# Adaptive-norm modulation in steps of 512 columns and a state-space recurrence whose backward half runs in reversed time, on one Trainium2 core

## The chip, the core and the metric

The kernel runs on one core of a Trainium2 chip. The core has a matrix engine (TensorE, PE in the rows), a vector engine (VectorE, DVE), an activation engine (ScalarE, ACT), GpSimd (POOL) and SyncE (SP), which here only issues loads. Each engine works through its own instructions in order and meets the others at semaphores. The metric is the device time of one execution in microseconds (us); smaller is better.

## What is computed

Two layers of a diffusion backbone, for 128 context tokens and 256 latent tokens (384 columns together), 1024 channels wide. Cut to what the change touches:

```python
def ada_mods(cvec, p):
    m = jax.nn.silu(cvec) @ p['ada_w'] + p['ada_b']          # 1024 x 6144 weights
    return jnp.split(m[:, None, :], 6, axis=-1)

def trunk_layer(x, cvec, p, mixer_fn):
    sh1, sc1, g1, sh2, sc2, g2 = ada_mods(cvec, p)
    mixed, extra = mixer_fn(rmsnorm(x, p['norm1_g']) * (1 + sc1) + sh1)
    x = x + g1 * mixed
    x = x + g2 * conv_ffn(rmsnorm(x, p['norm2_g']) * (1 + sc2) + sh2, p)
    return x, extra

# inside the mixer, beside three kinds of attention: a complex diagonal recurrence in both directions
for d, rev in enumerate((False, True)):
    a_re, a_im, bb_re, bb_im = s5_discretize(...)
    y_d, f_re, f_im = s5_direction(u, a_re, a_im, bb_re, bb_im, c_re, c_im, h0[:, d, 0], h0[:, d, 1], rev)
    y = y + y_d
```

The modulation is a product of two vectors (context and latent) with 1024 x 6144 weights in each layer. The recurrence has 16 groups of 64 complex states in each direction.

## The kernel before

One program handles both token sets at once: activations lie channel by channel, 128 channels on the partitions and 384 tokens along the free axis. A layer is a mixer (input projection, four head groups, output projection) and a gated MLP. Large products are done three times (`mm3`, L296 to L299): weights and activations are split into a high and a low part, and three matmuls of 384 or 386 columns add up. `split1` makes the two parts of a weight piece, the high one on ACT (L289), the low one on DVE (L290).

**Modulation.** The weights of a third of a layer's modulation (group g, 1024 x 2048) are loaded by SP in 16 pieces of 128 x 1024 (512 KB), into three buffers of the tag `ada`. `ada_steps` (L315 to L333) is a generator: one step loads a piece and issues four fp32 matmuls of 256 columns on it, whose 32-column stationary operands stand in the four column quarters of the array, so that four weights columns are worked on at once (L320). There are five such groups (80 steps); the sixth, the first third of layer 0, is done at the start in `first` by `mod` (L1413) on tiles of the tag `a0`, of which there are `NA0`.

**Recurrence.** Time is cut into steps of eight tokens, `NC` = 51 columns with pads. The forward direction lies on partitions 0 to 63, the backward one on 64 to 127. For each of four blocks of four groups, `states` (L774) multiplies the block's input with a table (eight fp32 matmuls of 51 columns with a 128 x 128 stationary operand, L779), rotates the result (L789 to L791), puts in the initial states, and runs four `tensor_tensor_scan` on DVE: real and imaginary part, forward (L797) and backward from the end (L799), on 64 partitions each. `outputs` (L814) turns states into tokens. The rotation and decay tables are made once in each layer by `s5_rot` (L644), which copies three of them with ACT (L659 to L661); layer 0's are made in the prologue, layer 1's during the MLP of layer 0.

**Order.** In the prologue (`first`) PE, ACT, DVE and SP follow the order of the code. In the mixer a string (`SPEC[l]`) sets which generator takes its next step: A is a modulation step, G a projection, N, Q and M the attention groups, S the recurrence, T its tables. Within that a scheduler places instructions by priorities; `adjacent` keeps a list of matmuls next to each other. Loads on SP and on GpSimd's queue start in order, each when its buffer is free.

Of the kernel before, what the change touches and what calls it, by code (L numbers as in the profile page):

```python
# [12 lines left out]
F32 = mybir.dt.float32  # L13
F32R = mybir.dt.float32r
I32 = mybir.dt.int32
AF = mybir.ActivationFunctionType
OP = mybir.AluOpType
# [3 lines left out]
L = 2  # L21
# [8 lines left out]
NC = 51  # L30
# [27 lines left out]
NA0 = 5  # L58
# [3 lines left out]
NADA = 3  # L62
# [7 lines left out]
SPEC = ['AATGTATAGGGTTTTGTATAGGGNGAGAANAGGNASNANNNASNAGAAASNGSATNSAANMGGNAGASQANSSQMQSAAAQMAMQAQMQMSAMAAAQASNQAAQQMQMAMAAAQSSSAQMMMMMAAAQMMAMAAAAM', 'SGAGAGSGASGAASNSGGSSGSNAGSAGAGNSSMNNANNGSNNGANSGQGNQASAMGAAQQGQNQQMNMQAQNMMQMAAAMAAQQQMAMQMAQAAAMMAM']  # L70
# [59 lines left out]
def _prepare(a):  # L130
    f = np.float32
    a = {n: np.asarray(v) for n, v in a.items()}
# [5 lines left out]
    def col(v, p=128):  # L138
        return v.reshape(-1, p).T

    r = {}
# [4 lines left out]
    r["ada"] = np.stack([w.reshape(8, 128, 4, 2, 256).transpose(0, 3, 1, 2, 4)  # L146
                         for l in range(L) for w in np.split(a["ada_w"][l], 3, axis=1)][1:]
                        ).reshape(5, 8, 2, 128, 1024)
# [69 lines left out]
def _program(tc, I, O):  # L218
# [95 lines left out]
    def ada_steps(l, g):  # L314
        acc = pa()  # L315
        for kc in range(8):
            for h in range(2):
                raw = piece(I["ada"][3 * l + g - 1, kc, h], 1024, "ada")
                for c in range(4):
                    PE.matmul(acc[32 * c:32 * c + 32, 256 * h:256 * h + 256], cw[:, kc],  # L320
                              raw[:, 256 * c:256 * c + 256], start=kc == 0 and h == 0,
                              stop=kc == 7 and h == 1)
                if kc < 7 or h == 0:
                    yield
        ar = kp.tile([128, 512], F32, name="ar", tag="sqz", bufs=3)
# [318 lines left out]
    def s5_rot(l, w, w4, qp, cmp):  # L644
# [14 lines left out]
        A.activation(w4[0], w[0], AF.Copy)  # L659
        A.activation(w4[1], w[1], AF.Copy)  # L660
        A.activation(w4[2], w[1], AF.Copy, scale=-1.0)  # L661
# [4 lines left out]
        V.memset(rt[64:128, :, 17:51:33], 0.0)  # L666
# [75 lines left out]
    def s5_steps(l, st, sp_):  # L742
# [28 lines left out]
        def states(b):  # L771
# [4 lines left out]
            for i in range(2):  # L776
                for g in range(4):
                    q = 4 * i + g
                    PE.matmul(e[:, NC * q:NC * q + NC], E[:, 128 * q:128 * q + 128], U[:, 4 * b + g], start=True,  # L779
                              stop=True)  # L780
# [12 lines left out]
            V.tensor_copy(t1[64:128, :, :, 50], HR[l][64:128, :, gs])  # L793
            gt = tmp("g")
            r3 = W[:, 3].rearrange("p g m -> p (g m)")
            for i in range(2):
                V.tensor_tensor_scan(gt[0:64, i].rearrange("p g m -> p (g m)"), r3[0:64],  # L797
# [777 lines left out]
```

## Time and profile before

| | |
|---|---|
| median of 3 runs | 1107.12 us (1101.26 to 1111.03) |
| the profiled execution's own time | 1107.33 us |
| its span | 1105.5 us |
| PE busy | 1065.4 us, 96% of the span |
| DVE busy | 795.7 us, 72% |
| ACT busy | 580.7 us, 53% |
| POOL busy | 88.3 us, 8% |

The span is the time from the first to the last instruction of one execution. Busy time of an engine counts each moment once, also where several of its instructions overlap. An fp32 matmul stands in the trace as two records, one of the split products and a transpose as one.

### The profile page before, as it was taken

How to read it: one execution, taken by the hardware profiler on the slowest of the kernel's cores; microseconds unless marked ns; L12 is line 12 of the kernel's file. 1: busy time of each engine (PE TensorE's matmuls, PEld its weight loads, DVE VectorE, ACT ScalarE, POOL GpSimd, SP SyncE). 2: the span in 40 equal slices, each digit the busy share in tenths (PEclk: the TensorE clock that was granted, in tenths of full speed). 3: DMA queues.
4: the chain of work that ended last, by engine and by line, in shares of the span. 5: the costliest groups of instructions: out<-in, count | busy, mean ns of one | idle time of the engine just before them, and what ended most of it. 6: DMA issues, size and time to landing. Idle time of an engine off the chain costs nothing.

```text
span 1105.5 us, 18673 instructions
## 1 busy us (share of the span) xinstructions
PE 1065.4 (96%) x6724; PEld 909.4 (82%) x6724; DVE 795.7 (72%) x1998; ACT 580.7 (53%) x1251; POOL 88.3 (8%) x201
## 2 busy tenths in 40 slices
PE   6798999999999999999999989899999999999998
PEld 3587475457999999999999877545799999999998
DVE  6897476778899864678966877557769775476753
ACT  3753445545676543455556645574568553355532
POOL 4212221000100000001110210100000000000000
PEclk8999898999999999999999999999999999999999
DMA  9987776555545334445455774436333434534343
GB/s 337 304 283 282 200 227 219 168 186 201 166 146 179 120 100 142 135 132 150 144 137 158 215 249 136 106 130 215 101 117 97 134 116 118 148 120 129 111 134 99
DMA packets 64700, 182.19 MB, mean 165 GB/s; under 512 B 15840, under 2 KB 19168, under 8 KB 64608
## 3 DMA queue, kind: packets, MB, share of 16 engines
q1 hardware_dynamic: 55456, 152.52, 44.1%
q0 software_dynamic: 8576, 28.16, 8.4%
q8 instruction: 53, 0.87, 0.3%
q10 hardware_dynamic: 576, 0.32, 0.1%
q14 instruction: 39, 0.32, 0.1%
HBM read 166.19 MB, written 14.78 MB: 164 GB/s over the span
## 4 chain that ended last, share of the span: by engine, by line
PE 81%; DMA 6%; DVE 6%; issue 4%; ACT 2%; POOL 1%; SPq 0%; DVEq 0%; POOLq 0%; ACTq 0%
PE pz L297 12%; PE pz L299 12%; PE pz L298 12%; PE psc L299 9%; PE psc L298 8%; PE psc L297 8%; PE pa L320 4%; PE psc L955 3%; DMA raw<-ada 2%; PE ptr L959 1%; PE po L974 1%; DMA tbw<-sw 1%; PE psc L779 1%; DVE lo L290 1%; DMA sf<-ca 1%
## 5 line engine op out<-in xcount | busy, mean ns | idle before, releaser
L289 ACT ACTIVATE hi<-raw 128x512 fp32r<-128x512 f32 (+2 forms) x396 | 228.1, 585 | 275.4 <-PE pz L298 111.9
L290 DVE TENSOR_TENSOR lo<-raw,hi 128x512 fp32r<-128x512 f32 (+2 forms) x396 | 250.8, 636 | 147.9 <-ACT hi L289 105.0
L299 PE MATMUL pz<-ah,lo 128*128 128x386 f32 (+1 forms) x616 | 211.6, 344 | 3.3 <-DVE lo L290 3.2
L297 PE MATMUL pz<-ah,hi 128*128 128x386 f32 (+1 forms) x616 | 214.7, 350 | 0.1
L298 PE MATMUL pz<-al,hi 128*128 128x386 f32 (+1 forms) x616 | 212.7, 346 | 0.0
L297 PEld LDWEIGHTS pz<-ah,hi 128*128 128x128 f32 x616 | 117.5, 191 | 15.7 <-issue 12.7
L299 PEld LDWEIGHTS pz<-ah,lo 128*128 128x128 f32 x616 | 117.6, 191 | 8.8 <-issue 4.5
L298 PEld LDWEIGHTS pz<-al,hi 128*128 128x128 f32 x616 | 117.9, 191 | 3.6 <-issue 2.1
L299 PE MATMUL psc<-ah,lo 128*128 128x386 f32 (+1 forms) x336 | 114.7, 341 | 0.1
L298 PE MATMUL psc<-al,hi 128*128 128x386 f32 (+1 forms) x336 | 114.8, 342 | 0.0
L297 PE MATMUL psc<-ah,hi 128*128 128x386 f32 (+1 forms) x336 | 114.7, 341 | 0.0
L299 PEld LDWEIGHTS psc<-ah,lo 128*128 128x128 f32 x336 | 63.9, 190 | 1.0 <-DVE lo L290 0.4
L297 PEld LDWEIGHTS psc<-ah,hi 128*128 128x128 f32 x336 | 64.2, 191 | 0.3 <-ACT hi L289 0.3
L298 PEld LDWEIGHTS psc<-al,hi 128*128 128x128 f32 x336 | 64.2, 191 | 0.2 <-issue 0.2
L320 PE MATMUL pa<-raw,cw 128*32 128x256 f32 x640 | 60.1, 394 | 4.2 <-DMA raw<-ada 3.9
L297 PE MATMUL pz<-fh,hi 128*128 128x384 f32 x176 | 59.5, 338 | 0.1
L299 PE MATMUL pz<-fh,lo 128*128 128x384 f32 x176 | 59.4, 338 | 0.0
L297 PE MATMUL psc<-fh,hi 128*128 128x384 f32 x176 | 59.4, 338 | 0.0
L299 PE MATMUL psc<-fh,lo 128*128 128x384 f32 x176 | 59.3, 337 | 0.0
L298 PE MATMUL pz<-fl,hi 128*128 128x384 f32 x176 | 59.2, 336 | 0.0
L298 PE MATMUL psc<-fl,hi 128*128 128x384 f32 x176 | 59.1, 336 | 0.0
L932 ACT ACTIVATE P<-P,ty 128x384 f32<-128x384 f32 (+1 forms) x72 | 38.9, 540 | 37.1 <-DVE P L931 25.5
(425 smaller groups left out, 1937.0 us busy)
## 6 DMA issues: line engine op xcount, KB each, us to landing
raw<-wup SPq DMA_DIRECT2D x88, 512.0 KB, 3.6
raw<-ada SPq DMA_DIRECT2D x80, 512.0 KB, 4.5
raw<-win SPq DMA_DIRECT2D x30, 512.0 KB, 5.0
raw<-wdn SPq DMA_DIRECT2D x32, 384.0 KB, 3.1
raw<-wdn SPq DMA_DIRECT2D x32, 320.0 KB, 2.9
a<-ada SPq DMA_DIRECT2D x16, 512.0 KB, 6.2
raw<-wout SPq DMA_DIRECT2D x16, 512.0 KB, 3.6
se<-tbo POOLq DMA_DIRECT2D x16, 256.0 KB, 3.6
```

What stands on the lines that cost most here:

```text
L289: A.activation(hi[:, :n], raw[:, a:b], AF.Copy)
L290: V.tensor_tensor(lo[:, :n], raw[:, a:b], hi[:, :n].bitcast(F32), op=OP.subtract)
L297: PE.matmul(out, wh, xh, start=start, stop=False)
L298: PE.matmul(out, wh, xl, start=False, stop=False)
L299: PE.matmul(out, wl, xh, start=False, stop=stop)
L320: PE.matmul(acc[32 * c:32 * c + 32, 256 * h:256 * h + 256], cw[:, kc], raw[:, 256 * c:256 * c + 256], start=kc == 0 and h == 0, stop=kc == ...
L779: PE.matmul(e[:, NC * q:NC * q + NC], E[:, 128 * q:128 * q + 128], U[:, 4 * b + g], start=True, stop=True)
L932: A.activation(P[:, :w], P[:, :w], AF.Exp, bias=mn, scale=-1.0, accum_out=rs)
L955: PE.matmul(S[:, :T], qf(1 + qb), kf(128, 512), start=True, stop=True)
L959: PE.transpose(tr[:, 128 * kb:128 * kb + 128], P[:, 128 * kb:128 * kb + 128], ident)
L974: calls.append(lambda kb=kb, j=j: PE.matmul(o[64 * j:64 * j + 64, 128:T], heads[j][2](1 + kb), PTs[j][1][:, kb].rearrange("p q c -> p (q c ...
```

## The change

Modulation: `ada_steps` now waits for the two pieces of a row of weights and then issues four matmuls of 512 columns, kept adjacent, every second step; the host packs the weights to suit. Prologue: of the 16 tiles of the first modulation third every third one goes to the buffers of the tag `ada`, the others to four (five before) of the tag `a0`. Recurrence: the backward half is held in reversed time. The table matmul is split into two of 64 stationary columns, the second reading the input backwards; one scan over all 128 partitions takes the place of a forward and a backward one; the rotation tables are copied in halves, the upper one reversed; the result is turned back where it is read. Both strings of `SPEC` are new.

```diff
@@ -55,7 +55,7 @@
 LAG = 2
 LATE = 7
 CM2 = 0
-NA0 = 5
+NA0 = 4
 NAH = 9
 NPT = 3
 NRAW = 3
@@ -67,7 +67,7 @@
 LNP = ()
 LOWP = 300
 LOWA = 3000
-SPEC = ['AATGTATAGGGTTTTGTATAGGGNGAGAANAGGNASNANNNASNAGAAASNGSATNSAANMGGNAGASQANSSQMQSAAAQMAMQAQMQMSAMAAAQASNQAAQQMQMAMAAAQSSSAQMMMMMAAAQMMAMAAAAM', 'SGAGAGSGASGAASNSGGSSGSNAGSAGAGNSSMNNANNGSNNGANSGQGNQASAMGAAQQGQNQQMNMQAQNMMQMAAAMAAQQQMAMQMAQAAAMMAM']
+SPEC = ['TTAGTGTAATTGTAATAGAGGTNAAAGGANAANGGNNAGAGAGSGANNSSAAANMNGSASQNNNNNTSGAAAQAGASSMQQSAMMQQMQASAMQAQMMSAQMAQASQAQAAAQMSMAASAAMMAMMMAMQMAMAAAA', 'SSSAAGAGAAGGSSGGASNSGASNAGGSGGSSMNNSANNGNNGQNANSGQNASAMGAAQQQQMNMQGMNQAGAMMAAQAAAQNQQMQMAQMMAQMAAAMM']
 
 WIN_COLS = [
     np.arange(768, 896), np.arange(896, 1024),
@@ -143,9 +143,8 @@
     r["xT"] = pk(x.T)
     cc = np.stack([a["c_ctx"], a["c"][0]], 1)
     r["cT"] = pk(cc)
-    r["ada"] = np.stack([w.reshape(8, 128, 4, 2, 256).transpose(0, 3, 1, 2, 4)
-                         for l in range(L) for w in np.split(a["ada_w"][l], 3, axis=1)][1:]
-                        ).reshape(5, 8, 2, 128, 1024)
+    r["ada"] = np.stack([w.reshape(8, 128, 2, 1024).transpose(0, 2, 1, 3)
+                         for l in range(L) for w in np.split(a["ada_w"][l], 3, axis=1)][1:])
     r["ada0"] = a["ada_w"][0][:, :2048].reshape(2, 4, 128, 2, 8, 128).transpose(4, 0, 2, 1, 3, 5).reshape(8, 2, 128, 1024)
     r["win"] = np.stack([np.stack([pk(a["w_in"][l][:, c]) for c in WIN_COLS]
                                   + [pk(a["w_in"][l][h * 512:(h + 1) * 512, 512:768]) for h in range(2)])
@@ -314,14 +313,16 @@
     def ada_steps(l, g):
         acc = pa()
         for kc in range(8):
+            raw = []
             for h in range(2):
-                raw = piece(I["ada"][3 * l + g - 1, kc, h], 1024, "ada")
-                for c in range(4):
-                    PE.matmul(acc[32 * c:32 * c + 32, 256 * h:256 * h + 256], cw[:, kc],
-                              raw[:, 256 * c:256 * c + 256], start=kc == 0 and h == 0,
-                              stop=kc == 7 and h == 1)
-                if kc < 7 or h == 0:
+                raw.append(piece(I["ada"][3 * l + g - 1, kc, h], 1024, "ada"))
+                if h == 0:
                     yield
+            adjacent([lambda c=c: PE.matmul(acc[32 * c:32 * c + 32], cw[:, kc],
+                                            raw[c // 2][:, 512 * (c % 2):512 * (c % 2) + 512], start=kc == 0,
+                                            stop=kc == 7) for c in range(4)])
+            if kc < 7:
+                yield
         ar = kp.tile([128, 512], F32, name="ar", tag="sqz", bufs=3)
         V.tensor_copy(ar, acc)
         tr = pt()
@@ -656,14 +657,14 @@
             yield from cmul_steps([v[:, :, h + 1:h + 1 + n] for v in w], [v[:, :, 1:1 + n] for v in w],
                                   [v[:, :, h:h + 1].to_broadcast(shp) for v in w], shp, cmp)
             h += n
-        A.activation(w4[0], w[0], AF.Copy)
-        A.activation(w4[1], w[1], AF.Copy)
-        A.activation(w4[2], w[1], AF.Copy, scale=-1.0)
+        for v, u, c in ((w4[0], w[0], 1.0), (w4[1], w[1], 1.0), (w4[2], w[1], -1.0)):
+            A.activation(v[0:64], u[0:64], AF.Copy, scale=c)
+            A.activation(v[64:128], u[64:128, :, ::-1], AF.Copy, scale=c)
         rt = w4[3]
         V.tensor_copy(rt, rho[:, lg, None].to_broadcast([128, 16, NC]))
         yield
         V.memset(rt[0:64, :, 0:18:17], 0.0)
-        V.memset(rt[64:128, :, 17:51:33], 0.0)
+        V.memset(rt[64:128, :, 0:34:33], 0.0)
         yield
         for i in range(4):
             G.dma_start(SW[l][:, :, 4 * NC * i:4 * NC * i + 4 * NC], w4[i].rearrange("p (b g) m -> p b (g m)", b=4))
@@ -776,8 +777,9 @@
             for i in range(2):
                 for g in range(4):
                     q = 4 * i + g
-                    PE.matmul(e[:, NC * q:NC * q + NC], E[:, 128 * q:128 * q + 128], U[:, 4 * b + g], start=True,
-                              stop=True)
+                    for d in range(2):
+                        PE.matmul(e[64 * d:64 * d + 64, NC * q:NC * q + NC], E[:, 128 * q + 64 * d:128 * q + 64 * d + 64],
+                                  U[:, 4 * b + g, ::1 - 2 * d], start=True, stop=True)
             e4 = e[:, :w8].rearrange("p (i g m) -> p i g m", i=2, g=4)
             wc = W[:, 0:1].to_broadcast([128, 2, 4, NC])
             ws = W[:, 1:3]
@@ -790,21 +792,18 @@
             V.tensor_tensor(t2, e4[:, ::-1], ws, op=OP.mult)
             V.tensor_tensor(t1, t1, t2, op=OP.add)
             V.tensor_copy(t1[0:64, :, :, 17], HR[l][0:64, :, gs])
-            V.tensor_copy(t1[64:128, :, :, 50], HR[l][64:128, :, gs])
+            V.tensor_copy(t1[64:128, :, :, 0], HR[l][64:128, :, gs])
             gt = tmp("g")
             r3 = W[:, 3].rearrange("p g m -> p (g m)")
             for i in range(2):
-                V.tensor_tensor_scan(gt[0:64, i].rearrange("p g m -> p (g m)"), r3[0:64],
-                                     t1[0:64, i].rearrange("p g m -> p (g m)"), 0.0, op0=OP.mult, op1=OP.add)
-                V.tensor_tensor_scan(gt[64:128, i].rearrange("p g m -> p (g m)")[:, ::-1], r3[64:128, ::-1],
-                                     t1[64:128, i].rearrange("p g m -> p (g m)")[:, ::-1], 0.0, op0=OP.mult,
-                                     op1=OP.add)
+                V.tensor_tensor_scan(gt[:, i].rearrange("p g m -> p (g m)"), r3,
+                                     t1[:, i].rearrange("p g m -> p (g m)"), 0.0, op0=OP.mult, op1=OP.add)
             t1, t2 = tmp("1"), tmp("2")
             V.tensor_tensor(t1, gt, wc, op=OP.mult)
             V.tensor_tensor(t2, gt[:, ::-1], ws, op=OP.mult)
             S = sp_.tile([128, 2, 4, NC], F32, name="S", tag="S", bufs=2)
             V.tensor_tensor(S[0:64, :, :, 1:NC], t1[0:64, :, :, 0:NC - 1], t2[0:64, :, :, 0:NC - 1], op=OP.subtract)
-            V.tensor_tensor(S[64:128, :, :, 0:NC - 1], t1[64:128, :, :, 1:NC], t2[64:128, :, :, 1:NC],
+            V.tensor_tensor(S[64:128, :, :, 0:NC - 1], t1[64:128, :, :, NC - 2::-1], t2[64:128, :, :, NC - 2::-1],
                             op=OP.subtract)
             A.activation(fin[0:64, :, gs], S[0:64, :, :, 17], AF.Copy)
             A.activation(fin[64:128, :, gs], S[64:128, :, :, 0], AF.Copy)
@@ -1400,7 +1399,8 @@
         H, W, wr, aw = [], [], [], []
 
         def load(k):
-            aw.append([up.tile([128, 1024], F32, name="a0", tag="a0", bufs=NA0) for p in range(2)])
+            aw.append([up.tile([128, 1024], F32, name="a0", tag="a0", bufs=NA0) if (2 * k + p) % 3 else
+                       wp.tile([128, 1024], F32, name="raw", tag="ada", bufs=NADA) for p in range(2)])
             for p in range(2):
                 SY.dma_start(aw[k][p], I["ada0"][k, p])
             if k % 2 == 0:
```

In the order of the built programs, PE in layer 0's mixer near its end, before: `pa` is the modulation's accumulator, `psc<-mk,mq` are attention scores, `ptr<-cst,P` transposes of softmax tiles, `pz<-ah,hi` a product of the split kind.

```order
L877 MATMUL pz<-g_1833,wglu 128x384 x2
L948 MATMUL ptr<-cst,P 128x128
L320 MATMUL pa<-raw,cw 32x256 x8
L959 MATMUL ptr<-cst,P 128x128 x6
L320 MATMUL pa<-raw,cw 32x256 x4
L955 MATMUL psc<-mk,mq 128x384 x2
L948 MATMUL ptr<-cst,P 128x128
L297 MATMUL pz<-ah,hi 128x384
L298 MATMUL pz<-al,hi 128x384
L320 MATMUL pa<-raw,cw 32x256 x4
L945 MATMUL psc<-mk,mq 128x128
```

The same stretch of PE now; `po<-PT,mv` is a product of softmax with values.

```order
L321 MATMUL pa<-raw,cw 32x512 x4
L958 MATMUL ptr<-cst,P 128x128 x6
L954 MATMUL psc<-mk,mq 128x384
L944 MATMUL psc<-mk,mq 128x128
L298 MATMUL pz<-ah,lo 128x384
L973 MATMUL po<-PT,mv 64x256 x6
L977 MATMUL po<-PT,mv 64x128 x2
L947 MATMUL ptr<-cst,P 128x128
L321 MATMUL pa<-raw,cw 32x512 x4
```

Steps of one piece in unequal numbers have become sets of four wider matmuls with other work between. In the whole program before, the 320 matmuls of L320 stand in 76 stretches (15 of one matmul, 2 of two, 10 of three, 29 of four, 4 each of five and seven, 7 of eight, 2 of nine, 3 of eleven); now 160 matmuls stand in 40 stretches of four.

PE at the recurrence's table product of one block in layer 0, before:

```order
L1122 MATMUL ptr<-cst,gvT 128x128 x3
L320 MATMUL pa<-raw,cw 32x256 x7
L779 MATMUL psc<-U,tbef 128x51 x8
L320 MATMUL pa<-raw,cw 32x256 x4
L955 MATMUL psc<-nkT,nqT 128x384
```

and the product of the same kind now:

```order
L762 MATMUL ptr<-cst,Zg 128x48 x8
L944 MATMUL psc<-nkT,nqT 128x128
L954 MATMUL psc<-nkT,nqT 128x384
L781 MATMUL psc<-U,tbef 64x51 x16
L298 MATMUL pz<-ah,lo 128x384
```

Eight matmuls of a block are sixteen; over the program they stand in 10 stretches in both orders.

ACT in the prologue, where layer 0's rotation tables are copied (`w<-rw`) between the modulation copies (`ar<-pa`) of two channel blocks and the next weight split:

```order
 L1416 ACTIVATE ar<-pa 128x256
-L659 ACTIVATE w_433<-rw 128x816
-L660 ACTIVATE w_434<-rw 128x816
-L661 ACTIVATE w_435<-rw 128x816
-L289 ACTIVATE hi<-raw 128x512
+L661 ACTIVATE w_433<-rw 64x816
+L662 ACTIVATE w_433<-rw 64x816
+L661 ACTIVATE w_434<-rw 64x816
+L662 ACTIVATE w_434<-rw 64x816
+L661 ACTIVATE w_435<-rw 64x816
+L662 ACTIVATE w_435<-rw 64x816
+L288 ACTIVATE hi<-raw 128x512
```

Six copies of 64 partitions stand where three of 128 stood.

## Rows read from the trace of the kernel before

**Rows 1.** Windows, from:to: length, busy us by engine (PE, PEld, DVE, ACT, POOL), granted clock, DMA.
```profile
57.00:265.00 208.00, 196.86 (x1438) 125.46 (x1436) 149.27 (x419) 101.07 (x246) 29.86 (x44) 0.95 0.69 219
620.00:785.00 165.00, 156.84 (x1063) 103.97 (x1062) 114.30 (x336) 86.98 (x212) 15.93 (x20) 0.99 0.55 167
119.40:129.60 10.20, 10.20 (x30) 5.70 (x26) 3.48 (x12) 1.94 (x6) 4.29 (x9) 0.50 0.65 205
```

**Rows 2.** Costliest groups on PE and DVE: busy us, mean ns of one.
```profile
L320 PE MATMUL pa<-raw,cw 128*32 128x256 f32 x640 | 60.1, 394 | 4.2 <-DMA raw<-ada 3.9
L799 DVE TENSOR_TENSOR_SCAN mg<-tbw,m 64x204 f32<-64x204 f32 x16 | 11.4, 710 | 0.2
L797 DVE TENSOR_TENSOR_SCAN mg<-tbw,m 64x204 f32<-64x204 f32 x16 | 9.2, 574 | 0.3
```

**Rows 3.** Timeline of PE late in layer 0's mixer: start us, us, records (x).
```profile
252.55 0.64 PE L320 MATMUL pa<-raw,cw 128*32 128x256 f32 x8
253.12 1.56 PE L955 MATMUL psc<-mk,mq 96*128 96x384 f32 x4
...
257.11 1.51 PE L974 MATMUL po<-PT,mv 128*64 128x256 f32 x12
258.45 0.39 PE L978 MATMUL po<-PT,mv 128*64 128x128 f32 x4
258.77 0.55 PE L959 MATMUL ptr<-cst,P 128*128 128x128 f32 x3
259.25 0.62 PE L320 MATMUL pa<-raw,cw 128*32 128x256 f32 x2
259.80 0.55 PE L959 MATMUL ptr<-cst,P 128*128 128x128 f32 x3
...
260.39 1.50 PE L320 MATMUL pa<-raw,cw 128*32 128x256 f32 x22
261.81 0.59 PE L955 MATMUL psc<-mk,mq 96*128 96x384 f32 x1
```

**Rows 4.** Timeline of PE: two modulation steps between split products.
```profile
68.87 0.33 PE L299 MATMUL pz<-ah,lo 128*128 128x384 f32 x1
69.13 1.07 PE L320 MATMUL pa<-raw,cw 128*32 128x256 f32 x16
70.13 0.45 PE L297 MATMUL pz<-ah,hi 128*128 128x384 f32 x1
```

**Rows 5.** Timeline of PE: matmuls on parts of the array; the table product.
```profile
67.99 0.67 PE L723 MATMUL ptr<-ca,bb 64*32 64x128 f32 x32
...
159.68 0.64 PE L832 MATMUL psc<-tbef,S 128*49 128x128 f32 x8
160.12 0.31 PE L829 MATMUL psc<-M,U 128*49 128x128 f32 x2
...
175.53 1.99 PE L779 MATMUL psc<-U,tbef 128*128 128x51 f32 x16
```

**Rows 6.** Timeline of ACT in the prologue.
```profile
41.10 0.89 ACT L659 ACTIVATE w<-rw 128x816 f32<-128x816 f32 x1 [1.54 <-DVE rw L491]
...
43.33 0.86 ACT L661 ACTIVATE w<-rw 128x816 f32<-128x816 f32 x1
44.10 0.61 ACT L289 ACTIVATE hi<-raw 128x512 fp32r<-128x512 f32 x1
```

**Rows 7.** Timeline of PE: a wait of the prologue and one of each mixer.
```profile
46.60 0.44 PE L1422 MATMUL ptr<-cst,ar 128*128 128x128 f32 x2 [3.25 <-ACT ar L1416]
...
118.81 0.64 PE L320 MATMUL pa<-raw,cw 128*32 128x256 f32 x8 [2.01 <-DMA raw<-ada]
...
641.49 0.77 PE L993 MATMUL ptr<-cst,rb 128*128 128x128 f32 x3 [2.10 <-DVE m L792]
```

**Rows 8.** DMA issues of modulation pieces, windows 57:130, 200:265: count, KB, us to landing.
```profile
raw<-ada SPq DMA_DIRECT2D x14, 512.0 KB, 5.9
raw<-ada SPq DMA_DIRECT2D x21, 512.0 KB, 4.3
```

## The prediction

> **What bounds the kernel now.** I read the page first: PE is busy 96% of the span (table above), DVE 72%, so an edit counts by what it takes off PE's row of work, or by a wait that it gives PE. Then the windows by stage [rows 1]: both places where modulation and recurrence run are the mixers, 57 to 265 us and 620 to 785 us. PE idles there 208.0 - 196.9 = 11.1 us and 165.0 - 156.8 = 8.2 us, while DVE has 149 of 208 us and 114 of 165 us. PE stays the bound with some 20 us taken off it. The two MLP stages between and after hold hardly a modulation step and no recurrence. Third, the timeline of PE, step by step: the time that a group takes from the row of work is not its own length (matmuls overlap with the next ones) but the distance from its start to the next start. Last, the waits of PE and the DMA list, since the change makes PE wait for two pieces at a time.
>
> The sum is made against the profiled execution, 1107.33 us, which is the median of the three runs (1107.12) within 0.02%.
>
> **Modulation on PE.** From the distances: eight records (four matmuls of 256 columns) take 253.12 - 252.55 = 0.57 us; two records, a matmul alone, 259.80 - 259.25 = 0.55, because the other three quarters of the array stand empty; twenty-two records 261.81 - 260.39 = 1.42 [rows 3]; sixteen 70.13 - 69.13 = 1.00 [rows 4]. Three matmuls then cost about 0.57, as four do. With the stretches counted in the order: 17 of one or two matmuls x 0.55 = 9.4; 39 of three or four x 0.57 = 22.2; 15 of five, seven or eight x 1.0 = 15.0; 5 of nine or eleven x 1.42 = 7.1; together 53.7 us. Now there are 40 sets of four with 512 columns. Such a set streams as many columns through each quarter as sixteen records do now, so 1.00 us, 40.0 us together. That is -13.7 us. Each stretch also has an edge: a split product streams 384 columns, 0.16 us at 2.4 GHz, and a modulation step behind it starts after 0.26 [rows 4]; 36 stretches fewer are -3.6, if all of them had this edge. By the group's busy time instead, 60.1 us [rows 2] against 40 x 1.07 [rows 4], it would be -17.3. I take **-16**, bounds -13.7 and -17.3. It is all on PE's row, so on the path.
>
> **Recurrence on PE.** A block's table product takes 1.99 us for 16 records, 0.12 each [rows 5], though only 51 columns stream: the load of 128 stationary columns sets it. Eight blocks are 15.9 us. Now a block has 32 records of 64 stationary columns in two halves of the array. No row has this shape. The nearest is L832, 49 stationary columns in two halves, at (160.12 - 159.68) / 8 = 55 ns a record [rows 5], where 128 columns stream: 32 x 55 ns = 1.76 us, eight blocks 14.1, so -1.8. The other end is L723 with 32 stationary columns in eight parts, 0.67 / 32 = 21 ns [rows 5]: 5.4 us, so -10.5. With 51 columns to stream it should lie below L832's pace, since half the stationary columns load beside the other half's work. I take **-4**, bounds +2.5 and -10.5.
>
> The plus end comes from the edges: a modulation stretch has 0.26 - 0.16 at its head, and its first four matmuls cost 0.57 where four more in the same stretch cost 1.00 - 0.57 = 0.43, together 0.24 us [rows 3, 4]. The ten stretches of table products now also run on parts of the array, 10 x 0.24 = +2.4, and if the halves gained nothing this would be left. The Trainium skill speaks against the split here: "TensorEngine Tiling (Array Packing)", Key Properties, says that a change of tiling mode drains TensorE. The 0.24 us of the modulation's edges agree with such a drain; by that rule alone the term would be +2.4, with L832's pace +0.6.
>
> **Recurrence on DVE.** Sixteen pairs of scans, 574 and 710 ns [rows 2], become sixteen scans over 128 partitions. DVE's time goes with elements per partition, so 16 x 574 = 9.2 us against 20.6: -11.4 us on DVE, less about 1 if the reversed read of the state costs what it costs the scan (710 against 574, eight instructions). DVE is not the bound; it counts where PE waits for what is queued behind a block's chain. PE waits 2.10 us at 641.49 for instructions behind the block's copy L792 [rows 7], and each block's chain is now 1.3 to 1.4 us shorter, of eight blocks one such place shows. I take **-1.5**, bounds 0 and -4.
>
> **Prologue on ACT.** The three copies stand 41.10 to 44.10, the last two 0.77 us apart [rows 6]. Six copies of 64 partitions and the same 816 elements take 6 x 0.79 = 4.7 us from 41.10, to 45.8. The split L289 and the modulation copy behind them on ACT come 1.7 us later, and PE waits for that copy already, 3.25 us [rows 7]. Nothing hides it: **+2**, bounds 0 (if the rest of the prologue has slack) and +2.7. Layer 1's six copies fall in the MLP, where PE has its split weights ahead: 0. The tiles `a0`: seven buffers in all instead of five bring pieces earlier, but PE's waits there name ACT, not DMA: 0.
>
> **Pairs of pieces.** Three buffers hold a set's two pieces and one more. The second piece of the next set gets a buffer when this set ends, 1.07 us after its start, and lands 4.3 us after its issue, 5.9 us in the busy early stretch [rows 8]: the next set can start 5.4 us (7.0) after this one. In the order of the change the two sets shown lie, by the distances in rows 3, 1.00 + six transposes 0.95 + a score product 0.75 + a short one and a split product 0.52 + values 1.34 + 0.32 + a transpose 0.16 = 5.0 us apart: PE would wait 0.4 us, and all behind it, since PE works in order. Counted so, 22 of the 38 distances within a mixer lie between 4.2 and 5.6 us, and the shortfalls to 5.4 add up to 6.6 us. Waits that PE has anyway for softmax or DVE take some of it, the early stretch adds some; the wait before, 2.01 us at 118.81 [rows 7], may go. I take **+6**, bounds 0 and +20.
>
> **Both lists.** The new orders move the other waits too. PE's 19 us of idle time in the mixers and the stretch at half clock, 119.4 to 129.6 [rows 1], worth 5 us, could go or double; I know no reason for either: 0, bounds -12 and +12.
>
> **The sum:** -16 - 4 - 1.5 + 2 + 6 = -13.5; 1107.3 - 13.5 = **1094 us**.
>
> **The rivals.**
> *Pairs eat the gain.* If pieces land as in the early stretch, each of the 22 close sets waits up to 1 us, +20 instead of +6: 1094 + 14 = 1108. For it: distances so near to the landing time, and only one piece in hand. Against: late in the mixers DMA has less to do and lands in 4.3 [rows 8].
> *Slower: pairs and the clock.* The granted clock stands at its lower level, 1.2 GHz, from 119.4 to 129.6, right after the wait of 2.01 us for a piece [rows 1, 7]. If the waits of the rival above bring 30 us more at half clock, 15 us of work is lost on top: 1108 + 15 = 1123. It decides when waits of 1 us and more follow each other every five us. Against: layer 1's mixer has 8.2 us of idle time and still a mean granted clock of 0.99 [rows 1].
> *Lists that fit.* If the orders also remove the waits for pieces (0 instead of +6) and half of what is idle or slow in the mixers (-9), 1094 - 15 = 1079.
> *The wider set is no cheaper.* If four matmuls of 512 columns cost two of today's sets apart, 1.14 us, modulation gains 5.6 us less: 1100. Sixteen records at 1.00 speak against it; it lies within the forecast's range.
>
> **Chances.** Forecast, 1085 to 1101: 0.52. Pairs eat the gain, 1101 to 1115: 0.24. Slower with the clock: 0.09. Lists that fit, below 1085: 0.15. Leaving out the slower rival and the outer part of the next two gives a range of 1080 to 1109. A difference of 1%, 11 us, is about what a measurement of this kernel can tell from none. Faster by more (below 1096): 0.15 + 0.42 of the forecast's 0.52 = 0.57; within 1%: 0.34; slower: 0.09.
>
> **What would show it.** PE: 320 records of modulation in 40 stretches, 1.0 us from start to next start; table products below 1.76 us a block; 16 scans of 128 partitions at 0.57 us; the prologue's wait for ACT 1.7 us longer; waits of PE for modulation pieces of 0.2 to 0.8 us each. I am wrong if these waits exceed 15 us in all, if the half-clock stretches of the mixers grow, or if a set takes 1.1 us and more.

## The result and the profile after

The changed kernel takes 1090.03 us (median of 4 runs, 1087.58 to 1092.82), beside 1106.76 us (1101.26 to 1111.03) for the kernel before in the same comparison: a ratio of 0.9875, 95% interval 0.9837 to 0.9913. That is 4 us below the forecast of 1094 and inside its range. The profiled execution took 1088.87 us, with a span of 1087.1 us.

First the windows by stage, of the kernel before. The columns are those of [rows 1] (PEld is PE's weight load); the stages are the prologue, layer 0's mixer and layer 1's mixer, each up to the statistics of the next norm.

```profile
0.00:56.50 56.50, 41.10 (x257) 26.91 (x258) 44.33 (x187) 30.63 (x64) 20.23 (x66) 0.89 0.91 322
56.50:284.20 227.70, 216.56 (x1556) 143.86 (x1555) 167.78 (x477) 113.58 (x278) 32.51 (x51) 0.95 0.68 218
596.30:803.20 206.90, 198.69 (x1321) 142.65 (x1321) 145.96 (x426) 117.79 (x286) 19.10 (x30) 0.99 0.54 162
```

The same stages of the kernel after.

```profile
0.00:56.50 56.50, 38.90 (x247) 24.24 (x248) 39.23 (x175) 32.11 (x65) 19.34 (x64) 0.88 0.88 325
56.50:276.70 220.20, 200.51 (x1446) 132.42 (x1445) 171.28 (x491) 119.31 (x286) 34.55 (x55) 0.98 0.72 232
586.30:784.30 198.00, 190.39 (x1267) 136.23 (x1266) 137.03 (x418) 116.93 (x286) 18.12 (x30) 0.97 0.54 167
```

A stage's length less PE's busy time is PE's idle time, and one less the granted clock, times the length, is what the clock cost. Layer 0's mixer is 7.5 us shorter, although PE idles 19.7 us there against 11.1; the clock cost 0.02 x 220.2 = 4.4 us against 0.05 x 227.7 = 11.4; so PE's work fell by about 9. Layer 1's mixer is 8.9 us shorter: idle 7.6 against 8.2, clock 5.9 against 2.1, work about 12 less. The clock has two decimals, so each of these work figures is good to 1 or 2 us. Ahead of 56.50 PE does 2.8 us less work than before (32.1 us against 34.9, by the same account), which then stands in the window of layer 0's mixer. The span fell by 18.4 us, and 16.4 of it lie in these two stages.

Then the groups on PE and DVE that answer to [rows 2]: busy us, mean ns of one, PE's idle time ahead of the group.

```profile
L321 PE MATMUL pa<-raw,cw 128*32 128x512 f32 x320 | 45.4, 633 | 6.7 <-DMA raw<-ada 6.6
L781 PE MATMUL psc<-U,tbef 128*64 128x51 f32 x256 | 9.8, 225 | 1.1 <-ACT P L927 0.6 <-DMA tbef<-se 0.4
...
L799 DVE TENSOR_TENSOR_SCAN mg<-tbw,m 128x204 f32<-128x204 f32 x16 | 8.6, 569 | 0.2
```

PE's waits for modulation pieces rose from 3.9 us to 6.6. The scans fell from 20.6 us to 8.6, with 569 ns for 128 partitions where 64 had taken 574.

The timeline of PE shows the prices by distance, as [rows 3 to 5] did: sets of the modulation late in layer 0's mixer, and a block's table product.

```profile
155.69 1.14 PE L781 MATMUL psc<-U,tbef 128*64 128x51 f32 x32
156.76 0.44 PE L298 MATMUL pz<-ah,lo 128*128 128x384 f32 x1
...
237.38 1.07 PE L321 MATMUL pa<-raw,cw 128*32 128x512 f32 x8
238.37 0.49 PE L944 MATMUL psc<-mk,mq 96*128 96x128 f32 x2
...
242.47 1.06 PE L321 MATMUL pa<-raw,cw 128*32 128x512 f32 x8
243.47 0.88 PE L958 MATMUL ptr<-cst,P 128*128 128x128 f32 x6
...
247.34 1.07 PE L321 MATMUL pa<-raw,cw 128*32 128x512 f32 x8
...
253.23 1.06 PE L321 MATMUL pa<-raw,cw 128*32 128x512 f32 x8 [1.21 <-DMA raw<-ada]
...
257.97 1.06 PE L321 MATMUL pa<-raw,cw 128*32 128x512 f32 x8
```

A set takes 0.99 to 1.00 us (238.37 - 237.38, 243.47 - 242.47), and over the whole program, each set from its start to the next instruction's start and less PE's idle time in between, 42.8 us where the steps before took 55.0, sets at half clock included in both. What a set costs the instruction ahead of it is not in this measure. The table product of a block takes 156.76 - 155.69 = 1.07 us, 33 ns a record; eight blocks come to 8.9 us, against 14.6 before by the same measure. The sets follow each other after 5.1, 4.9, 5.9 and 4.7 us, and one of these four had to wait for its piece. The pieces land as they did [rows 8], by the same view and windows, 57 to 130 and 200 to 265 us:

```profile
raw<-ada SPq DMA_DIRECT2D x16, 512.0 KB, 5.6
raw<-ada SPq DMA_DIRECT2D x21, 512.0 KB, 4.3
```

Last the prologue, ACT's copies and PE's waits, which answer to [rows 6] and the first line of [rows 7].

```profile
41.21 0.89 ACT L661 ACTIVATE w<-rw 64x816 f32<-64x816 f32 x1 [1.54 <-DVE rw L492]
...
45.74 0.89 ACT L662 ACTIVATE w<-rw 64x816 f32<-64x816 f32 x1
46.66 0.63 ACT L288 ACTIVATE hi<-raw 128x512 fp32r<-128x512 f32 x1
...
49.17 0.69 PE L1422 MATMUL ptr<-cst,ar 128*128 128x128 f32 x2 [5.70 <-ACT ar L1416]
...
56.34 0.44 PE L1422 MATMUL ptr<-cst,ar 128*128 128x128 f32 x2 [1.14 <-ACT ar L1416]
```

Six copies, 0.91 us from start to start, hold the next split until 46.66; it stood at 44.10. PE's wait grew from 3.25 us to 5.70.

### The profile page after: what moved, and what is told of

The parts are those of the page before. It is cut to its first block, busy times and chain, and to the rows that moved or that the text cites. A ratio compares the mean times of both kernels' runs of the same rounds, so it can differ in the third digit from the quotient of the medians.

```text
span 1087.1 us, 18268 instructions
## 1 busy us (share of the span) xinstructions
PE 1036.8 (95%) x6532; PEld 889.2 (82%) x6532; DVE 782.0 (72%) x1982; ACT 585.0 (54%) x1257; POOL 87.0 (8%) x201
## 4 chain that ended last, share of the span: by engine, by line
PE 80%; DMA 7%; DVE 5%; ACT 3%; issue 2%; POOL 1%; SPq 1%; DVEq 0%; POOLq 0%; ACTq 0%
PE pz L296 13%; PE pz L298 12%; PE pz L297 12%; PE psc L298 9%; PE psc L297 9%; PE psc L296 9%; DMA bias<-rpb 3%; PE pa L321 3%; DMA raw<-ada 3%; PE psc L954 2%; PE ptr L958 1%; PE po L973 1%; DVE lo L289 1%; DMA sf<-ca 1%; PE psc L831 1%
## 5 line engine op out<-in xcount | busy, mean ns | idle before, releaser
L321 PE MATMUL pa<-raw,cw 128*32 128x512 f32 x320 | 45.4, 633 | 6.7 <-DMA raw<-ada 6.6
L931 ACT ACTIVATE P<-P,ty 128x384 f32<-128x384 f32 (+1 forms) x72 | 38.8, 540 | 20.6 <-DVE P L930 16.7
```

The source lines that it names most:

```text
L321: adjacent([lambda c=c: PE.matmul(acc[32 * c:32 * c + 32], cw[:, kc], raw[c // 2][:, 512 * (c % 2):512 * (c % 2) + 512], start=kc == 0, st ...
L931: A.activation(P[:, :w], P[:, :w], AF.Exp, bias=mn, scale=-1.0, accum_out=rs)
```

## The experiments

The first theory was the one of the prediction: the two parts, modulation and recurrence, take their time off PE, and the lists are worth nothing by themselves. Its rival: the lists carry the gain, or make it possible. Four kernels undo one thing or do one thing alone.

**Modulation alone** (`ada_steps` and its packing as in the change, all else as before):

```diff
+            raw = []
             for h in range(2):
-                raw = piece(I["ada"][3 * l + g - 1, kc, h], 1024, "ada")
...
+                raw.append(piece(I["ada"][3 * l + g - 1, kc, h], 1024, "ada"))
...
+            adjacent([lambda c=c: PE.matmul(acc[32 * c:32 * c + 32], cw[:, kc],
+                                            raw[c // 2][:, 512 * (c % 2):512 * (c % 2) + 512], start=kc == 0,
+                                            stop=kc == 7) for c in range(4)])
```

> The kernel before with the modulation alone in sets of four matmuls of 512 columns; recurrence, prologue tiles and both lists as before. Theory P (the parts: PE work taken off its row makes the gain): 40 sets of 1.00 us instead of 76 stretches take 12 us off PE, and the old lists, which were not spaced for pairs of pieces, give 2 to 6 us of it back as waits for pieces: 1097 to 1101 us, 6 to 10 below the kernel before. Theory L (the lists make the gain, the parts alone lose theirs to waits): within 3 us of the kernel before, or slower.

Measured: 1108.86 us, ratio 1.0076 (1.0045 to 1.0107). It is slower, although its sets cost 42.1 us by distance, as little as in the kernel after. Its windows, layer 0's mixer, layer 1's mixer and a stretch of the first:

```profile
56.50:296.90 240.40, 219.85 (x1381) 141.34 (x1379) 170.88 (x488) 114.73 (x280) 34.19 (x53) 0.91 0.67 218
608.80:807.60 198.80, 190.54 (x1199) 138.32 (x1199) 145.91 (x426) 117.58 (x286) 18.26 (x30) 0.99 0.51 161
123.40:143.90 20.50, 20.50 (x57) 9.58 (x56) 8.28 (x34) 7.80 (x21) 4.28 (x9) 0.50 0.56 175
```

and PE's timeline ahead of that stretch and in it:

```profile
119.37 0.52 PE L994 MATMUL ptr<-cst,rb 128*128 128x128 f32 x3 [0.78 <-DVE rb L991]
122.14 1.06 PE L321 MATMUL pa<-raw,cw 128*32 128x512 f32 x8 [2.25 <-DMA raw<-ada]
...
139.65 1.94 PE L321 MATMUL pa<-raw,cw 128*32 128x512 f32 x8
141.52 1.05 PE L758 MATMUL ptr<-cst,uT 128*48 128x128 f32 x4
```

Layer 1's mixer gained 8.1 us. Layer 0's lost 12.7: 9.4 more idle (20.6 against 11.1) and 10.3 more to the clock (0.09 x 240.4 = 21.6 against 11.4), less some 7 of work. PE waited 0.78 us for DVE and 2.25 for a piece, and then ran 20.5 us at 0.50, the lower level of 1.2 GHz; a set cost 141.52 - 139.65 = 1.87 us there.

**Recurrence alone** (the hunks of the copies, the table product, the scans and the read of the state, on the kernel before):

```diff
-                    PE.matmul(e[:, NC * q:NC * q + NC], E[:, 128 * q:128 * q + 128], U[:, 4 * b + g], start=True,
-                              stop=True)
+                    for d in range(2):
+                        PE.matmul(e[64 * d:64 * d + 64, NC * q:NC * q + NC], E[:, 128 * q + 64 * d:128 * q + 64 * d + 64],
+                                  U[:, 4 * b + g, ::1 - 2 * d], start=True, stop=True)
```

> The kernel before with the recurrence alone in reversed time (halved table products, one scan, copies in halves). Theory P: 5.7 us off PE's row in the table products, 2.5 us more in the prologue behind ACT's copies, about 1 us from shorter chains on DVE: 3 to 5 us below the kernel before, 1102 to 1104 us. Theory L: no change, within 2 us.

Measured: 1104.97 us, 1.0018 (0.9988 to 1.0049). No difference that can be measured, and the 3 to 5 us that the first theory expected lie outside the interval.

**Lists alone** (the new `SPEC` on the kernel before):

```diff
-SPEC = ['AATGTATAGGGTTTTGTATAGGGNGAGAANAGGNASNANNN...
+SPEC = ['TTAGTGTAATTGTAATAGAGGTNAAAGGANAANGGNNAGAG...
```

> The kernel before with the two new lists alone. Theory P: the lists were made for the new parts and move waits about, within 5 us of the kernel before. Theory L: 6 us or more below it, 1101 us or less.

Measured: 1105.12 us, 1.0024 (0.9999 to 1.0049). No gain.

**Both parts with the old lists** (the old `SPEC` on the kernel after):

```diff
-SPEC = ['TTAGTGTAATTGTAATAGAGGTNAAAGGANAANGGNNAGAG...
+SPEC = ['AATGTATAGGGTTTTGTATAGGGNGAGAANAGGNASNANNN...
```

> The changed kernel with the two old lists. Theory P: it keeps most of the gain, 1092 to 1097 us; the waits for pieces grow by 2 to 6 us over the changed kernel's 6.6. Theory L: it keeps less than half, 1099 us or more.

Measured: 1101.59 us, 0.9986 (0.996 to 1.0012), no difference from before, where with the new lists it was 0.9875. Its mixers:

```profile
56.50:280.90 224.40, 202.68 (x1448) 133.13 (x1446) 172.23 (x494) 118.99 (x285) 35.02 (x57) 0.97 0.70 230
589.80:793.70 203.90, 192.67 (x1269) 137.19 (x1268) 140.07 (x418) 117.79 (x286) 18.12 (x30) 0.97 0.50 162
```

They are 4.2 and 5.9 us longer than those of the kernel after: 2.0 and 3.6 of that are idle time of PE, and PE's waits for pieces are 9.3 us in the whole program, against 6.6. The rest is not clock: over the whole of these two executions the granted clock is 0.983 in both, PE idles 54.6 us against 50.3 and is busy 1041.5 us against 1036.8. About half of the 9.0 us by which the spans differ is idle time, and half is work on PE. (The medians differ by more, about 12 us; the granted clock of the other runs with the old lists lies between 0.975 and 0.985, that of the kernel after between 0.980 and 0.986.) So the first theory falls: the parts alone give 0.1%, the lists alone nothing, both together 1.25%.

Why do the parts need the lists? The theory from here on: a set waits for its second piece, since three buffers hold one set and one piece of the next, and the lists space the sets. The spacing is argued and not seen: counted without PE's idle time, 14 of 36 distances from set to set within a mixer are below 5.4 us in the kernel after, and 10 of 37 with the old lists. The waits can be tested: with one piece for a set, the lists should not matter. Three kernels use the first piece of a row twice; half of the modulation weights are neither loaded nor used, while PE's matmuls stay as many and as wide. Their order does not stay: sets now stand closer together, and in the third kernel some 820 of PE's 6532 records have another place than in the kernel after.

```diff
-                raw.append(piece(I["ada"][3 * l + g - 1, kc, h], 1024, "ada"))
+                raw.append(raw[0] if h else piece(I["ada"][3 * l + g - 1, kc, h], 1024, "ada"))
```

This edit on the kernel with the modulation alone, with both parts and old lists, and on the kernel after:

> The modulation-only kernel again, but a set loads one piece and uses it for both halves, so that half of the modulation weights is left out (its modulation is not the reference's) and a set never waits for a second piece; PE's work is the same. Theory W (what the parts gain is lost to waits of PE for the second piece and to the lower granted clock that follows them): the 11 us of waits for pieces and most of the 43 us at half clock in layer 0's mixer go; 1.0 to 1.8% below the kernel before. Rival O (the old list is bad for the parts in other ways, above all by where the sets stand between the attention's steps): within 0.4% of the kernel before.

> All parts with the old lists, one piece a set as above (half of the modulation weights left out). Theory W: as fast as the changed kernel with one piece a set, within 0.4%, so 1.3 to 2% below the kernel before. Rival O: it stays 0.8% or more above the changed kernel with one piece a set.

> The changed kernel, one piece a set as above (half of the modulation weights left out). Theory W: its 6.6 us of waits for pieces go and part of them comes back elsewhere: 0.3 to 0.6% below the changed kernel, so 1.5 to 1.9% below the kernel before. Rival O: nothing over 0.2%, as its list hides the pieces already.

Measured: 1081.04 us, 0.9801 (0.9776 to 0.9826); 1081.73 us, 0.9821 (0.9797 to 0.9846); 1078.99 us, 0.9787 (0.9764 to 0.981). The first of them is the kernel that had lost 0.8%: its waits for pieces, 25.5 us over 18 times on PE and its weight load with both pieces (11.1 us on PE alone), are a single one of 0.6 us here. All three gain about 2%, the first and the third more than was expected, and what the lists add fell from 1.1 points to 0.3, with intervals that overlap. That fits the waits. But these kernels also load 20 MB less, so it could be the amount; a later kernel tells that apart. It could be the order too; no kernel here tells that apart.

**Two pieces, 256 columns** (the pairs of the change, with eight narrow matmuls in place of four wide ones):

```diff
-            adjacent([lambda c=c: PE.matmul(acc[32 * c:32 * c + 32], cw[:, kc],
...
+            calls = [lambda h=h, c=c: PE.matmul(acc[32 * c:32 * c + 32, 256 * h:256 * h + 256], cw[:, kc],
+                                                raw[h][:, 256 * c:256 * c + 256], start=kc == 0 and h == 0,
+                                                stop=kc == 7 and h == 1) for h in range(2) for c in range(4)]
+            adjacent(calls[1:] + calls[:1])
```

> The changed kernel with eight adjacent matmuls of 256 columns in a set, four on each of its two pieces, in place of four of 512. By the rows before, sixteen records take 1.00 us as the wide set does. Theory P (the pairing of steps saves time, the width of the matmul does not): within 0.2% of the changed kernel, so 1.0 to 1.5% below the kernel before. Rival (the width saves it): 5 to 10 us above the changed kernel, at most 0.8% below the kernel before.

Measured: 1101.19 us, 0.9977 (0.9952 to 1.0002). The expectation missed, and the time lies on the side of its rival, some 11 us above the kernel after. Where eight matmuls stand together, the width itself costs nothing, as PE's timeline shows:

```profile
88.70 0.64 PE L322 MATMUL pa<-raw,cw 128*32 128x256 f32 x8 [0.20 <-DMA raw<-ada]
89.27 0.38 PE L297 MATMUL pz<-hi,ah 128*128 128x256 f32 x1
...
96.37 1.07 PE L322 MATMUL pa<-raw,cw 128*32 128x256 f32 x16
97.37 0.66 PE L707 MATMUL ptr<-cst,eb 128*128 128x128 f32 x4
```

Sixteen narrow records cost 97.37 - 96.37 = 1.00 us, as eight wide ones do. But the scheduler did not keep the eight matmuls together: 160 wide matmuls had stood in 40 stretches, these stand in 58, of which 36 hold eight records at 0.57 us, so that they take 46.3 us in all by distance, not 42.8. The waits for pieces, on PE and its weight load, came to 22.6 us over 18 times (15.8 over 13 in the kernel after). Its span is 11.8 us longer than that of the kernel after: by PE's busy time and the granted clock (0.978 against 0.983) some 5 of that are work, 5.7 clock and 1.2 idle time. What the wide form gives here is that a set stays whole; the run does not say what width alone is worth.

**The kernel after once more, and with a fourth buffer.** The kernel after was run again beside the last three, as it is. In the second, modulation has four buffers, with all weights loaded; the room (512 KB) comes from three tiles of the recurrence's output that move to another tag, and from three small buffers.

```diff
-NADA = 3
+NADA = 4
...
-    def tiny(shape, tag="tiny", bufs=10, dt=F32):
+    def tiny(shape, tag="tiny", bufs=7, dt=F32):
...
-            y = sp_.tile([128, T], F32, name="yT", tag="yT", bufs=1)
+            y = kp.tile([128, T], F32, name="yT", tag="sq", bufs=5)
```

> The changed kernel once more, timed beside the three others of this call: 1.0 to 1.5% below the kernel before.

> The changed kernel with four buffers for modulation pieces instead of three, all weights loaded. Room for the fourth comes from three small tiles of the recurrence (yT, ga, gs) that move into a tag which exists already, and from seven instead of ten buffers for the smallest tiles. Both pieces of the next set are then in hand while a set runs. Theory W: PE's waits for pieces fall from 15.8 us (matmuls and weight loads together) to 5 or less, 0.6 to 0.9% below the changed kernel, near the one-piece kernel's 2.1% below the kernel before. Rival D (the one-piece kernel gained from moving 20 MB less, not from waiting less): within 0.3% of the changed kernel.

Measured: the kernel after 1088.9 us, 0.9856 (0.9807 to 0.9906); four buffers 1083.44 us, 0.9804 (0.9754 to 0.9854). The mixers with four buffers:

```profile
56.50:269.50 213.00, 198.57 (x1442) 132.91 (x1441) 167.90 (x482) 114.55 (x280) 32.17 (x52) 0.98 0.70 232
580.30:778.30 198.00, 189.40 (x1267) 136.05 (x1266) 137.00 (x418) 117.00 (x286) 18.11 (x30) 0.97 0.53 164
```

and what its modulation waits for in the whole program (us, times; PE and its weight load together):

```profile
  DMA raw<-ada: 7.0, 6
```

Layer 0's mixer is 7.2 us shorter than in the kernel after and PE idles 14.4 us in it, not 19.7; layer 1's is the same to 0.1 us. So 5.3 us of idle time went (3.9 against the second execution of the kernel after, which idles 18.3), and the medians differ by 5.5 us. All weights are loaded, so the smaller amount is not needed for the gain. That it is the wait alone is not shown: with the fourth buffer the scheduler also put some 750 of PE's 6532 records in other places, four of its stretches are two sets in a row, and tiles moved to make room. This is the fastest kernel of the study that computes everything, ahead of both kernels. Its interval against the kernel before overlaps that of the kernel after, but the two ran side by side, and five of the six runs of the kernel after lie above all six of this one.

**Four buffers, and the reversed copies on DVE:**

```diff
-            A.activation(v[64:128], u[64:128, :, ::-1], AF.Copy, scale=c)
+            V.tensor_scalar(v[64:128], u[64:128, :, ::-1], c, None, op0=OP.mult)
```

> The kernel with four buffers, and in the rotation tables the three reversed upper copies on DVE instead of ACT. By the prediction's prologue term ACT's six copies hold the modulation copy behind them 2.5 us longer than three did, so PE's long wait in the prologue, 5.7 us, falls to 3.2 to 4.2 us and the kernel is 1 to 2 us below the one with four buffers alone. Rival: DVE's own queue there is as late, and the wait stays above 5 us with no gain.

Measured: 1083.44 us, 0.9813 (0.9768 to 0.9859), the same. ACT and PE in its prologue:

```profile
42.25 1.66 ACT L661 ACTIVATE w<-rw 64x816 f32<-64x816 f32 x2 [0.55 <-DVE rw L499]
43.81 0.61 ACT L288 ACTIVATE hi<-raw 128x512 fp32r<-128x512 f32 x1
...
48.80 0.50 ACT L1437 ACTIVATE ah<-xb,mods,ty 128x128 fp32r<-128x128 f32 x1 [2.02 <-DVE ty L1431]
...
46.31 0.44 PE L1422 MATMUL ptr<-cst,ar 128*128 128x128 f32 x2 [3.25 <-ACT ar L1416]
...
54.34 0.63 PE L1422 MATMUL ptr<-cst,ar 128*128 128x128 f32 x2 [2.73 <-ACT ar L1416]
```

PE's first wait is back at 3.25 us, and the split is at 43.81. But DVE now makes ACT wait 2.02 us further on, PE's second wait is 2.73 us (1.93 with four buffers alone), and it ends at 54.34, where with four buffers alone it ends at 56.00 (53.77 before). So 1.7 us come back in the prologue, where 2.5 were taken off the first wait. They don't show in the time: in the profiled executions layer 0's mixer ends 1.6 us later than with four buffers alone. The medians are equal, and the six runs of each kernel lie 5 to 6 us apart, so whether a part of the gain is left can't be told.

**Two scans again** (the kernel after, each scan split into two of 64 partitions, both forward):

```diff
-                V.tensor_tensor_scan(gt[:, i].rearrange("p g m -> p (g m)"), r3,
-                                     t1[:, i].rearrange("p g m -> p (g m)"), 0.0, op0=OP.mult, op1=OP.add)
+                for q in (slice(0, 64), slice(64, 128)):
+                    V.tensor_tensor_scan(gt[q, i].rearrange("p g m -> p (g m)"), r3[q],
+                                         t1[q, i].rearrange("p g m -> p (g m)"), 0.0, op0=OP.mult, op1=OP.add)
```

> The changed kernel with two scans on 64 partitions each in place of every scan on 128, both forward: 16 instructions of 0.57 us more on DVE, 9.1 us. By the prediction's term of 1.5 us (0 to 4) the kernel is 0 to 0.4% above the changed kernel. Rival (DVE's time is on the path in the mixers): 0.6 to 0.9% above it.

Measured: 1099.26 us, 0.995 (0.992 to 0.998), so 10.4 us, 0.95%, above the kernel after beside it. By the total that is the rival's side. Its mixers:

```profile
56.50:288.20 231.70, 206.58 (x1445) 136.07 (x1443) 180.11 (x500) 119.34 (x285) 35.48 (x57) 0.96 0.69 223
596.30:794.90 198.60, 189.22 (x1267) 135.34 (x1266) 141.95 (x426) 117.03 (x286) 18.10 (x30) 0.97 0.52 167
```

DVE has some 11 us more to do in scans. Layer 1's mixer pays 0.6 us for its share, with 1.8 us more of idle time on PE; layer 0's pays 11.5: 5.4 more idle and 4.9 more to the clock. The waits for modulation pieces, on PE and its weight load, are 21.8 us over 20 times. But some 170 of PE's 6532 records also stand in another order in this kernel, all but two of them in layer 0's mixer. There PE's waits for DVE are as long as in the kernel after (8.8 us against 8.7), and its waits for pieces are longer (9.5 against 6.7). So where the order stayed, the longer scans cost 0.6 us; what layer 0 lost stands beside the moved rows, and no run separates the two.

## Why the prediction was right

The total was right, to 4 us. It came about by terms that do not simply add, as the prediction had added them. This table, worked out from each profiled execution's span, PE's busy time and mean granted clock, shows PE's account for the whole program in us. Work is the busy time less what the clock took.

| kernel | span | PE busy | PE idle | granted clock | lost to the clock | work |
|---|---|---|---|---|---|---|
| before | 1105.5 | 1065.4 | 40.1 | 0.983 | 18.8 | 1046.6 |
| modulation alone | 1109.9 | 1059.4 | 50.5 | 0.972 | 31.1 | 1028.3 |
| recurrence alone | 1097.5 | 1051.7 | 45.8 | 0.989 | 12.1 | 1039.6 |
| both, old lists | 1096.1 | 1041.5 | 54.6 | 0.983 | 18.6 | 1022.9 |
| after | 1087.1 | 1036.8 | 50.3 | 0.983 | 18.5 | 1018.3 |

A second execution of the kernel after gives 1016.4 us of work, so the last column is good to some 2 us. The spans are those of single executions: that of the recurrence alone was the fastest of its runs.

**Modulation on PE, -16: -12.2 by distance, -18 by the table.** The price of a set, 1.00 us, was right. The edge, the -2.3 that I took on top of -13.7, stands ahead of a set, so a distance that begins with the set can't hold it. It is there: behind a split product a stretch starts after 0.26 us in both kernels (the median of nine places and of ten), where split products of 384 columns follow each other after 0.18, and there are 36 stretches fewer. The term was not too large; what the rest of the 18 consists of was not taken apart. The width did what the sixteen records of [rows 4] said.

**Recurrence on PE, -4: -5.7 by distance, -7 by the table.** 33 ns a record lies between the two rows that bounded it (21 and 55 ns), as it should if half of the columns load beside the other half's work. The Trainium skill has two rules on this in "TensorEngine Tiling (Array Packing)", Key Properties: a change of tiling mode drains TensorE, which I had weighed, and different tiles can load weights and multiply in parallel, which I had not cited. The sum went the way of the second, 1.07 us a block where [rows 5] have 1.99 us; no run here takes a drain apart from it.

**Prologue, +2: +2.6.** Right in mechanism, and within its bounds in size. I priced a copy at 0.79 us from the 0.77 of [rows 6], which is the distance from the last copy to the split behind it; the six copies stand 0.91 apart. They end at 46.6 instead of 45.8, PE's wait grew by 2.45, and its last wait ends 56.34 - 53.77 = 2.6 us later.

**Pairs of pieces, +6: +2.7 in PE's own waits.** The mechanism was the right one, and the risk that mattered most; the waits are fewer and longer than the 0.2 to 0.8 us forecast (five on PE, 1.3 us in the mean). On PE they stay below the 15 us that I had set as a sign of being wrong; with its weight load, which overlaps PE, they are 15.8 us, against 10.3 before. What was too long is the distance that a set needs, 5.4 us. I took the median landing, 4.3 us, which mixes two kinds of load. When a set ends, two buffers come free and two loads start, 0.42 us apart; the next set needs only the first, since its other piece is in the third buffer. Single loads in the windows 238.4 to 238.6, 238.92 to 239 and 248.4 to 248.6 us:

```profile
raw<-ada SPq DMA_DIRECT2D x1, 512.0 KB, 3.5
raw<-ada SPq DMA_DIRECT2D x1, 512.0 KB, 4.4
raw<-ada SPq DMA_DIRECT2D x1, 512.0 KB, 4.7
```

The first and second load behind the set at 237.38 landed after 3.5 and 4.4 us, so that a set can start 1.06 + 3.5 = 4.6 us after the one ahead of it. Sets did follow after 5.1, 4.9 and 4.7 us without a wait; the one that waited, at 253.23, had a first load of 4.7 us. The first kernel of the study shows the slower rival in kind, at about half its size: waits and then half clock in layer 0's mixer (1.0076, against 1123 / 1107 = 1.014 of the rival). With both parts and the new lists it did not come about, and a fourth buffer takes 5.5 us more off.

**Recurrence on DVE, -1.5: about -1, where it can be read.** In layer 1, with PE's order as it was but for one record, the scans put back cost 0.6 us and 1.8 us of idle time on PE; twice that lies within the bounds of 0 and -4. Layer 0's mixer lost 11.5 us by the same edit, but there the order moved, and PE's waits for DVE did not grow. The time lies in waits for pieces and in the clock, so these 11.5 us by themselves don't speak against the term. By itself, on the kernel before, the recurrence gave nothing that can be measured.

**Both lists, 0 within -12 and +12: about -12, given the parts.** This term was mis-sized, and for a reason that the prediction should have seen: I valued the lists by themselves, where they are indeed worth nothing (1.0024), and not together with the parts, though I had worked out how close the pairs stand. With the parts they save about as much work on PE as idle time (the last two lines of the table); what in the order does it stays open. The terms for pairs and lists can't be priced apart: both change how often PE meets a piece that is not there yet.

So the right total is in part luck. By the table 28 us of work came off PE, where 20 were forecast, and 10 us of idle time came on, where 6.5 were (the other three terms); the clock took the same. Both forecasts were too small, and they offset each other in part. And the lists, which I set at zero, made the difference between 0.9986 and 0.9875.

One reading was wrong without harm. I took the 710 ns of L799 in [rows 2] for the price of a reversed scan. It is a mean with one outlier, as the last section shows.

## What to carry to other kernels

When a step starts to consume two loads at once, ask how many buffers it holds against how many it needs, before counting what its wider matmuls save: here the same parts gave -2% with a new order and a fourth buffer, -1.25% with the new order alone, and -0.1% with neither; a fourth buffer under the old order was not run. Read idle time and granted clock by stage, since both can give back what PE saves: in the kernel with the modulation alone they took 20 us from one mixer. And test parts and orders together as well as one by one; none of the three gained alone. Where a scheduler sets the order, compare the order too before a difference is put down to the edit: a buffer more or a scan split in two moved PE's rows here.

## What the hardware showed beside that

A scan over 204 elements takes the same time on 64 partitions and on 128, and forward and reversed alike. The 710 ns come from one of sixteen scans, while the other fifteen take 579 or 580. DVE and GpSimd at that place in the kernel before:

```profile
625.32 3.35 POOL L1146 TENSOR_TENSOR bias<-bias,cst 128x1024 f32<-128x1024 f32 x1 [13.68 <-DMA bias<-rpb]
...
626.45 2.67 DVE L799 TENSOR_TENSOR_SCAN mg<-tbw,m 64x204 f32<-64x204 f32 x1
```

GpSimd's addition runs until 628.67 and the scan, begun within it, until 629.12, some 0.45 us later. In the kernel with two scans it is the same: one scan of 2.59 us begins at 156.99, GpSimd's addition runs from 156.50 to 159.13, and its 31 other scans take 554 to 580 ns. That one waits for the other is only read from these places; no run here tested it.

The second thing is ACT's price: copies of 816 elements took 0.89 us on 64 partitions, as on 128 [rows 6]. From start to start, copies of the lower and the reversed upper half in turn stand 0.91 us apart, and two copies of lower halves in a row 0.78 us ((43.81 - 42.25) / 2, in the last kernel but one); what makes the difference was not tested. Halves by partition cost a full instruction each, on ACT as on DVE, while on TensorE a block in two halves of 64 columns took 1.07 us instead of 1.99.
